# Token operands' low halves on VectorE, and a later load of the mixer's constants, in a two-layer decoder trunk

## The chip, the core and the metric

One core of one Trainium2 chip runs the whole kernel. The metric is the device time of one execution in microseconds; three runs of the kernel before are given by their median. The engines named here are TensorE (PE; its weight loads PEld), VectorE (DVE), ScalarE (ACT), GpSimd (POOL, which also issues transfers) and SyncE (SP, which here only issues transfers).

## The reference

Two layers, each a feed-forward sub-layer, a token mixer and a second feed-forward sub-layer, on x of 512 tokens by 1024 channels in float32:

```
h = rms_norm(x, g1);  x = x + 0.5 * (silu(h @ w_gate) * (h @ w_up)) @ w_down      # D_FF = 2816
h = rms_norm(x, g2);  q, k, v, u = split(h @ w_in)
    o = causal differential attention (4 heads, RoPE), rms_norm per head
    p = causal mean pooling of u over windows 2, 4, 8, 16, a linear map per group
    x = x + concat(o, p) @ w_out
h = rms_norm(x, g3);  x = x + 0.5 * (silu(h @ w_gate2) * (h @ w_up2)) @ w_down2
```

A final rms_norm follows the second layer.

## The kernel before, in words

Activations lie transposed: a partition is a channel, the free dimension holds the 512 tokens. Each matrix product is made of three matmuls of float32r halves (`mm3`, lines 95 to 97): a number t is split into hi, its rounding, and lo = t - hi, and the product is hi\*hi + hi\*lo + lo\*hi. So every operand, weight or token, needs a hi and a lo tile.

There are two ways to make them. `split` (lines 143 and 144) is a cast on ScalarE and a subtraction on VectorE. The way "by DMA" has ScalarE write -t, rounded, into lo, POOL issue a transfer that adds t to it as it lands, and ScalarE cast hi (lines 164 to 166 for weights, 359 to 361 for tokens). Weights come in blocks of 128 by 1024 through six raw tiles (`wraw`) and five hi and five lo tiles. `weights()` returns the next block and first starts the making of those up to four blocks ahead, with the loads of raw blocks three further ahead on SP's queue.

A feed-forward part (`ffn`) has 11 pairs of hidden blocks, in three groups of 4, 4 and 3; after each group a down projection of 8 blocks (`down`, 24 or 18 matmuls each) adds to x. The first pair of a part (the first two of the very first part) is `plain`: gate and up products straight from the normed x. During it the sum of squares becomes the row r, and `operands` makes the token operands of all other pairs. Those pairs, `mixed`, need seven products in place of eight: tokens are cut into halves and channels into even and odd, the weight blocks A11, A12, A21, A22 and sums of them (u1 to u4) are multiplied by b[1] to b[7], of which b[1] and b[2] are normed x itself (b11, b21), and the others b22 (b[3]) and the combinations e4, e5, e6, e7. A product is 24 matmuls of 128x256; the order is 1, 2, 6, 5, 7, 3, 4, with the weights A11, A12, u2, u1, u3, u4, A22. Products 1, 6, 7 and 4 add up in bank ps_a, 2 in ps_g, 5 and 3 in ps_c; between them ScalarE copies a bank out (p1, w, p5, with preference by `high_priority`) and VectorE adds it to another (g1, up2, g2). Product 6 goes on in ps_a and so needs p1 copied first. The blocks A11, A12 and A22 get their low halves by DMA; the sums get theirs by `split`.

Of the seven token operands b[1], b[2], b[6] and b[5] are made by `split`, and b[7], b[3], b[4] by DMA. `constants()` (lines 820 to 825) loads lam, cst (cosine and sine tables and pooling counts) and the causal mask on SP's queue and has VectorE cast the mask to bfloat16; it is called after the very first plain pair. The readers of these three are in `lambdas` and `mix`, after the first part.

The order of each engine's queue is fixed when the kernel is built, by the Tile scheduler: program order is the rank, and an instruction that is ready by the scheduler's estimate may go ahead of a better-ranked one that is not. On the chip every queue then runs strictly in that order.

Of the kernel before, what the change touches and what calls it, by code (L numbers as in the profile page):

```python
# [15 lines left out]
ALU = mybir.AluOpType  # L16
# [54 lines left out]
def trunk(ctx: ExitStack, tc: tile.TileContext, xT, gu1, dn1, win_qk, win_v, win_u, poolw, wout, gu2, dn2, small, lams, consts, outT):  # L71
    nc = tc.nc
# [8 lines left out]
    def arena(name, dt=F32R):  # L81
        return act.tile([P, 2, S], dt, tag="arena", name=name)
# [59 lines left out]
    def split(hi, lo, raw):  # L142
        nc.scalar.copy(hi, raw)  # L143
        nc.vector.tensor_sub(lo, raw, hi.bitcast(F32))  # L144
# [197 lines left out]
    def operands(norm, r):  # L342


        def quarter(name, dt=F32):
            return act.tile([P, 4, HS], dt, tag="arena", name=name)

        def h(odd, half):
            t = quarter("h")
            ts = slice(half * HS, (half + 1) * HS)  # L350
            for i in range(4):
                k = 2 * i + odd
                nc.vector.scalar_tensor_tensor(t[:, i, :], x[:, k, ts], sm[:, norm.gcol + k : norm.gcol + k + 1], r[:, ts], ALU.mult, ALU.mult)
            return t

        def parts(t, by_dma=False):
            hi, lo = quarter("bhi", F32R), quarter("blo", F32R)
            if by_dma:
                nc.scalar.mul(lo, t, -1.0)
                nc.gpsimd.dma_start(lo, t, accum_op=ALU.add)  # L360
                nc.scalar.copy(hi, t)
            else:
                split(hi, lo, t)
            return hi, lo

        b = {}
        b11 = h(0, 0)
        b[1] = parts(b11)
        b21 = h(1, 0)
        b[2] = parts(b21)  # L370
        b12 = h(0, 1)
        e5 = quarter("e5")
        nc.vector.tensor_sub(e5, b11, b12)
        b22 = h(1, 1)
        e6 = quarter("e6")
        nc.vector.scalar_tensor_tensor(e6, e5, -1.0, b22, ALU.mult, ALU.subtract)
        e4 = b21
        nc.vector.scalar_tensor_tensor(e4, e6, -1.0, b21, ALU.mult, ALU.subtract)
        b[6] = parts(e6)
        b[5] = parts(e5)  # L380
        e7 = b12
        nc.vector.tensor_sub(e7, b22, b12)
        b[7] = parts(e7, by_dma=True)
        b[3] = parts(b22, by_dma=True)
        b[4] = parts(e4, by_dma=True)
        return b

    def ffn(norm, l, nxt, first=None):
        st = {}
        hh, hl = [], []  # L390

        def hidden(u):

            hi, lo = arena("hhi"), arena("hlo")
            split(hi, lo, u)
            hh.append(hi)
            hl.append(lo)

        def plain(first, at):

            banks = [bank("ps_pl") for _ in range(4)]
            gates, u = [], pair32("u")

            def gated():
                if "b" not in st:
                    st["b"] = operands(norm, st["r"])
                for ps in banks[:2]:
                    s = single("silu")
                    nc.vector.tensor_mul(s, ps, st["r"])
                    nc.scalar.activation(s, s, AF.Silu)  # L410
                    gates.append(s)

            for q in range(8):
                if q == 0 and first:
                    first(banks[:2])
                if q == at:
                    st["rT"] = rms_cols(norm.ssum, 1.0 / D, pin=True)
                if q == at + 1:
                    st["r"] = rms_rows(st["rT"])
                if q < 4 and first:  # L420
                    continue
                blk, jj = divmod(q, 2)
                if jj == 0:
                    hi, lo = weights()
                ps = banks[blk // 2 * 2 + jj]
                for i in range(4):
                    c = slice((jj * 4 + i) * P, (jj * 4 + i + 1) * P)
                    mm3(ps, hi[:, c], lo[:, c], *norm.k(2 * i + blk % 2), blk % 2 == 0 and i == 0, blk % 2 == 1 and i == 3)
                if q == 6 and "r" in st:
                    gated()  # L430
            if not gates:
                gated()
            for jj in range(2):
                v = u[:, jj, :]
                nc.vector.scalar_tensor_tensor(v, banks[2 + jj], -1.0, st["r"], ALU.mult, ALU.mult)
                nc.vector.tensor_mul(v, v, gates[jj])
            hidden(u)

        def halves(t):
            return t.rearrange("p (j s) -> p j s", j=2)  # L440

        def mixed():

            b = st["b"]
            u = pair32("u")

            def product(q, ps, start):
                w = weights()
                for jj in range(2):
                    triples(ps[:, jj * HS : (jj + 1) * HS], w, b[q], jj, start and jj == 0, True, True)  # L450

            def copied(ps, name):
                t = single(name)
                with tc.high_priority(PRIO):
                    nc.scalar.copy(t, ps)  # L455
                return t

            a, g, c = bank("ps_a"), bank("ps_g"), bank("ps_c")
            product(1, a, True)
            p1 = copied(a, "p1")  # L460
            product(2, g, True)
            g1 = single("g1")
            with tc.high_priority(PRIO):
                nc.vector.tensor_add(g1, g, p1)
            nc.scalar.activation(g1, g1, AF.Silu)
            product(6, a, False)
            w = copied(a, "w")
            product(5, c, True)
            p5 = copied(c, "p5")
            product(7, a, False)  # L470
            up2 = single("up2")
            with tc.high_priority(PRIO):
                nc.vector.tensor_add(up2, a, p5)
            product(3, c, False)
            g2 = single("g2")
            with tc.high_priority(PRIO):
                nc.vector.tensor_add(g2, c, w)
            nc.scalar.activation(g2, g2, AF.Silu)
            product(4, a, False)
            with tc.high_priority(PRIO):  # L480
                nc.vector.tensor_mul(u[:, :, :HS], halves(a), halves(g1))
            nc.vector.tensor_mul(u[:, :, HS:], halves(up2), halves(g2))
            hidden(u)

        for hf, (q0, nq) in enumerate(PARTS):
            hh.clear()
            hl.clear()
            for q in range(q0, q0 + nq):
                if q >= plain_pairs(first):
                    mixed()  # L490
                elif q:
                    plain(None, -2)
                else:
                    plain(first, 6 if first else 2)
                    if first:
                        constants()

            def down(ps, n, part, ts=slice(0, S), midway=None):
                hi, lo = part
                for j in range(2 * nq):  # L500
                    if midway and j == nq:
                        midway()
                    c = slice(j * P, (j + 1) * P)
                    mm3(ps[:, ts], hi[:, c], lo[:, c], hh[j // 2][:, j % 2, ts], hl[j // 2][:, j % 2, ts], j == 0, j == 2 * nq - 1)
                nc.vector.scalar_tensor_tensor(x[:, n, ts], ps[:, ts], -0.5, x[:, n, ts], ALU.mult, ALU.add)  # L505

            tail = hf == len(PARTS) - 1
            last = tail and isinstance(nxt, Final)
            for n in range(KD - 2 if last else KD):
                down(bank("ps_dn"), n, weights())  # L510
                if tail:
                    nxt.add(n)
            if last:

                n = KD - 2
                parts = weights(), weights()
                first_half, second = slice(0, HS), slice(HS, S)
                for i in range(2):
                    down(bank("ps_dn"), n + i, parts[i], first_half)
                    nxt.add(n + i, first_half)  # L520
                down(bank("ps_dn"), n, parts[0], second, lambda: nxt.cols(first_half))
                nxt.add(n, second)
                down(bank("ps_dn"), n + 1, parts[1], second, nxt.rows)
                nxt.add(n + 1, second)
                nxt.finish(first_half)
                nxt.cols(second)
                nxt.rows()
                nxt.finish(second)
# [414 lines left out]
```

## Time and profile before

| | us |
|---|---|
| median of 3 runs (lowest, highest) | 1809.5 (1808.0, 1811.78) |
| profiled execution, its own time | 1807.46 |
| span of its trace | 1805.4 |
| TensorE busy | 1759.8 (97%) |
| VectorE busy | 1124.5 (62%) |
| ScalarE busy | 951.5 (53%) |
| GpSimd busy | 210.5 (12%) |

Busy shares are over the whole span; the mean granted TensorE clock was 0.988 of full speed. The profile names a group by line, engine, operation, and output tile <- input tiles. Buffer numbers are left out, so the token tiles b11, b21, b12 and b22 all appear as `h` (as do e7 and e4, which are written over b12 and b21), e5 and e6 as `e`, p1 and p5 as `p`. L143 and L144 are the two lines of `split` for all tiles.

### The profile page before, as it was taken

To read this page: it belongs to the slowest core of one execution; us is meant where nothing else is said; L and a number is where in the kernel's file an instruction comes from. 1 tells how busy PE (TensorE), PEld (TensorE's weight loads), DVE (VectorE), ACT (ScalarE), POOL (GpSimd) and SP (SyncE) were. 2 spreads that over 40 slices of the span, in tenths; PEclk is the share of its full clock that TensorE was granted. 3 is DMA by queue.
4 is the path that set the end of the run, shared out by engine and by line. 5 is a ranking of instruction groups with operands and counts; after the bars stand their busy time and mean duration, and the time that the engine had idled before them with its cause. 6 is when DMAs were issued, how large, how long until landed. Compare 5 with 4: busy or idle time off the path is not lost.

```text
span 1805.4 us, 26850 instructions
## 1 busy us (share of the span) xinstructions
PE 1759.8 (97%) x10936; PEld 1577.1 (87%) x10936; DVE 1124.5 (62%) x1495; ACT 951.5 (53%) x1298; POOL 210.5 (12%) x211
## 2 busy tenths in 40 slices
PE   9899999999999899999999999999999989999997
PEld 7889989877788889989889899898777879899896
DVE  5945646577967546646575466465788576465464
ACT  7635626545466526626565265264445666264453
POOL 1100001110022001001220010012100310010001
PEclk9999999999999999999999999999999999999999
DMA  9656746522236756737757466375122567376461
GB/s 277 164 141 148 190 103 162 151 65 74 70 102 134 181 134 155 188 89 166 186 119 185 116 164 187 94 167 149 39 74 71 149 126 193 90 181 173 115 155 47
DMA packets 73451, 246.95 MB, mean 137 GB/s; under 512 B 8048, under 2 KB 12784, under 8 KB 73328
## 3 DMA queue, kind: packets, MB, share of 16 engines
q1 hardware_dynamic: 52304, 169.18, 30.3%
q0 software_dynamic: 20880, 76.03, 23.6%
q8 instruction: 85, 1.39, 0.3%
q14 instruction: 38, 0.31, 0.1%
q10 hardware_dynamic: 144, 0.03, 0.0%
HBM read 236.82 MB, written 2.10 MB: 132 GB/s over the span
## 4 chain that ended last, share of the span: by engine, by line
PE 85%; DVE 6%; DMA 4%; issue 3%; ACT 1%; SPq 1%; POOL 1%; POOLq 0%; DVEq 0%; ACTq 0%
PE ps_dn L96 9%; PE ps_dn L95 9%; PE ps_dn L97 9%; PE ps_a L97 8%; PE ps_a L95 8%; PE ps_a L96 8%; PE ps_c L95 4%; PE ps_c L97 4%; PE ps_c L96 4%; PE ps_pr L95 2%; PE ps_pr L97 2%; PE ps_pr L96 2%; DMA wlo<-gu 2%; PE ps_g L95 2%; PE ps_g L96 2%
## 5 line engine op out<-in xcount | busy, mean ns | idle before, releaser
L143 ACT CAST whi<-wraw 128x1024 fp32r<-128x1024 f32 (+2 forms) x275 | 273.7, 997 | 458.1 <-PE ps_dn L96 143.8
L144 DVE TENSOR_TENSOR wlo<-wraw,whi 128x1024 fp32r<-128x1024 f32 (+2 forms) x275 | 317.5, 1156 | 114.1 <-ACT whi L143 113.3
L97 PE MATMUL ps_a<-bhi,wlo 128*128 128x256 f32 x1248 | 359.8, 288 | 15.5 <-DMA wlo<-gu 15.5
L95 PE MATMUL ps_a<-bhi,whi 128*128 128x256 f32 x1248 | 359.1, 288 | 5.3 <-ACT p L455 5.1
L96 PE MATMUL ps_a<-blo,whi 128*128 128x256 f32 x1248 | 359.7, 288 | 0.2
L96 PE MATMUL ps_dn<-hlo,whi 128*128 128x512 f32 (+1 forms) x716 | 276.6, 386 | 0.2 <-DVE hlo L144 0.2
L97 PE MATMUL ps_dn<-hhi,wlo 128*128 128x512 f32 (+1 forms) x716 | 276.0, 386 | 0.0
L95 PE MATMUL ps_dn<-hhi,whi 128*128 128x512 f32 (+1 forms) x716 | 275.7, 386 | 0.0
L97 PEld LDWEIGHTS ps_a<-bhi,wlo 128*128 128x128 f32 x1248 | 245.6, 197 | 16.3 <-DMA wlo<-gu 16.3
L95 PEld LDWEIGHTS ps_a<-bhi,whi 128*128 128x128 f32 x1248 | 245.3, 197 | 6.2 <-ACT p L455 5.3
L96 PEld LDWEIGHTS ps_a<-blo,whi 128*128 128x128 f32 x1248 | 245.2, 197 | 1.9 <-DMA blo<-h 1.0
L165 POOL DMA_DIRECT2D wlo<-gu x133 | 116.1, 875 | 1032.6 <-ACT wlo L164 800.0
L166 ACT CAST whi<-wraw 128x1024 fp32r<-128x1024 f32 x133 | 139.3, 1048 | 131.2 <-PE ps_dn L96 62.2
L505 DVE SCALAR_TENSOR_TENSOR x<-ps_dn,x 128x512 f32<-128x512 f32 (+1 forms) x98 | 66.6, 680 | 191.8 <-PE ps_dn L97 191.8
L95 PE MATMUL ps_c<-bhi,whi 128*128 128x256 f32 x624 | 177.2, 284 | 5.7 <-ACT bhi L143 5.7
L96 PE MATMUL ps_c<-blo,whi 128*128 128x256 f32 x624 | 177.4, 284 | 1.2 <-DMA blo<-h 1.0
L97 PE MATMUL ps_c<-bhi,wlo 128*128 128x256 f32 x624 | 176.9, 284 | 0.0
L96 PEld LDWEIGHTS ps_dn<-hlo,whi 128*128 128x128 f32 x716 | 134.5, 188 | 28.0 <-DVE hlo L144 1.6
L97 PEld LDWEIGHTS ps_dn<-hhi,wlo 128*128 128x128 f32 x716 | 134.5, 188 | 27.1
L95 PEld LDWEIGHTS ps_dn<-hhi,whi 128*128 128x128 f32 x716 | 134.5, 188 | 26.7
L164 ACT ACTIVATE wlo<-wraw 128x1024 fp32r<-128x1024 f32 x133 | 140.0, 1056 | 0.2 <-DMA wraw<-gu 0.2
L95 PEld LDWEIGHTS ps_c<-bhi,whi 128*128 128x128 f32 x624 | 120.2, 193 | 6.3 <-ACT bhi L143 6.3
(173 smaller groups left out, 3226.5 us busy)
## 6 DMA issues: line engine op xcount, KB each, us to landing
wraw<-gu SPq DMA_DIRECT2D x174, 512.0 KB, 3.8
wlo<-gu POOLq DMA_DIRECT2D x133, 512.0 KB, 7.1
wraw<-dn SPq DMA_DIRECT2D x64, 512.0 KB, 4.2
wraw<-dn SPq DMA_DIRECT2D x32, 384.0 KB, 3.4
wraw<-wqk SPq DMA_DIRECT2D x16, 512.0 KB, 3.6
wraw<-wo SPq DMA_DIRECT2D x16, 512.0 KB, 3.7
blo<-h POOLq DMA_DIRECT2D x12, 512.0 KB, 7.2
wraw<-wv SPq DMA_DIRECT2D x8, 512.0 KB, 3.7
```

The lines of the kernel that those rows point to most:

```text
L95: nc.tensor.matmul(out, a_hi, b_hi, start=start, stop=False, skip_group_check=more)
L96: nc.tensor.matmul(out, a_hi, b_lo, start=False, stop=False, skip_group_check=more)
L97: nc.tensor.matmul(out, a_lo, b_hi, start=False, stop=stop, skip_group_check=more)
L143: nc.scalar.copy(hi, raw)
L144: nc.vector.tensor_sub(lo, raw, hi.bitcast(F32))
L164: nc.scalar.mul(lo[:, :n], raw[:, :n], -1.0)
L165: nc.gpsimd.dma_start(lo[:, :n], src, accum_op=ALU.add)
L166: nc.scalar.copy(hi[:, :n], raw[:, :n])
L505: nc.vector.scalar_tensor_tensor(x[:, n, ts], ps[:, ts], -0.5, x[:, n, ts], ALU.mult, ALU.add)
```

## The change

The token operands b[7], b[3] and b[4] are made by `split` like the other four: ScalarE casts hi, VectorE subtracts. And `constants()` is called no longer after the first plain pair but after the four pairs of the first group, ahead of its down projection.

```
-        def parts(t, by_dma=False):
+        def parts(t):
             hi, lo = quarter("bhi", F32R), quarter("blo", F32R)
-            if by_dma:
-                nc.scalar.mul(lo, t, -1.0)
-                nc.gpsimd.dma_start(lo, t, accum_op=ALU.add)
-                nc.scalar.copy(hi, t)
-            else:
-                split(hi, lo, t)
+            split(hi, lo, t)
             return hi, lo
...
-        b[7] = parts(e7, by_dma=True)
-        b[3] = parts(b22, by_dma=True)
-        b[4] = parts(e4, by_dma=True)
+        b[7] = parts(e7)
+        b[3] = parts(b22)
+        b[4] = parts(e4)
...
                     plain(first, 6 if first else 2)
-                    if first:
-                        constants()
...
             last = tail and isinstance(nxt, Final)
+            if first and hf == 0:
+                constants()
             for n in range(KD - 2 if last else KD):
                 down(bank("ps_dn"), n, weights())
```

## Rows read from the trace of the kernel before

**Rows 1.** Page, part 1: busy us (share of span) and instructions by engine.

```profile
PE 1759.8 (97%) x10936; PEld 1577.1 (87%) x10936; DVE 1124.5 (62%) x1495; ACT 951.5 (53%) x1298; POOL 210.5 (12%) x211
```

**Rows 2.** TensorE's waits, whole span: total us, times, longest us.

```profile
PE ps_a L97 <- DMA wlo<-gu: 15.5, 4, 4.9
...
PE ps_c L95 <- ACT bhi L143: 5.7, 3, 1.9
...
PE ps_a L95 <- ACT p L455: 5.1, 1, 5.1
```

**Rows 3.** Windows, four places: length, busy by engine, granted clock, DMA share, GB/s.

```profile
58.64:85.85 27.21, 20.44 (x147) 20.09 (x145) 23.89 (x29) 21.00 (x26) 5.25 (x6) 0.87 0.91 212
571.53:601.23 29.70, 22.75 (x146) 21.79 (x145) 18.65 (x21) 18.42 (x21) 5.17 (x6) 0.83 0.74 162
930.35:959.89 29.54, 22.61 (x146) 21.56 (x145) 18.34 (x21) 18.41 (x21) 5.19 (x6) 0.83 0.74 163
1465.58:1493.86 28.28, 21.24 (x146) 20.32 (x145) 18.04 (x21) 18.52 (x21) 5.22 (x6) 0.88 0.78 170
```

**Rows 4.** TensorE timeline: start, length, what; first matmuls of two products.

```profile
604.11 0.28 PE L95 MATMUL ps_a<-bhi,whi 128*128 128x256 f32 x1
...
607.00 0.28 PE L95 MATMUL ps_c<-bhi,whi 128*128 128x256 f32 x1
```

**Rows 5.** Windows behind or around waits, columns as in rows 3.

```profile
63.90:69.80 5.90, 5.90 (x27) 5.90 (x28) 5.14 (x8) 5.68 (x8) 0.00 (x0) 0.50 1.06 211
78.30:85.85 7.55, 5.89 (x50) 5.68 (x48) 5.77 (x8) 3.56 (x4) 0.00 (x0) 1.00 1.03 238
592.94:599.00 6.06, 6.06 (x28) 6.06 (x29) 0.96 (x2) 1.04 (x1) 0.00 (x0) 0.50 0.83 206
932.50:937.20 4.70, 4.68 (x25) 4.59 (x26) 4.67 (x5) 3.34 (x4) 1.73 (x2) 0.64 0.38 60
```

**Rows 6.** VectorE timeline, first part; brackets: idle before it, what ended it.

```profile
38.61 1.23 DVE L175 TENSOR_TENSOR wsum<-wraw 128x1024 f32<-128x1024 f32 x1 [3.81 <-DMA wraw<-gu]
...
44.50 0.23 DVE L825 CAST maskb<-mask 128x128 bf16<-128x128 f32 x1 [4.66 <-DMA mask<-consts]
```

**Rows 7.** Timeline of ScalarE, first feed-forward part.

```profile
54.74 1.05 ACT L143 CAST bhi<-e 128x1024 fp32r<-128x1024 f32 x1 [3.88 <-DVE e L376]
...
63.27 0.57 ACT L455 COPY p<-ps_a 128x512 f32<-128x512 f32 x1
```

**Rows 8.** DMA issues: count, KB each, median us from issue to landing.

```profile
wlo<-gu POOLq DMA_DIRECT2D x133, 512.0 KB, 7.1
...
cst<-consts SPq DMA_DIRECT2D x1, 520.0 KB, 12.2
...
mask<-consts SPq DMA_DIRECT2D x1, 64.0 KB, 19.0
```

**Rows 9.** Timeline of ScalarE, second feed-forward part.

```profile
574.09 1.05 ACT L359 ACTIVATE blo<-h 128x1024 fp32r<-128x1024 f32 x1
...
578.47 0.59 ACT L455 COPY w<-ps_a 128x512 f32<-128x512 f32 x1 [1.44 <-PE ps_a L97]
...
582.27 2.02 ACT L164 ACTIVATE wlo<-wraw 128x1024 fp32r<-128x1024 f32 x2
```

**Rows 10.** Timeline of POOL, second feed-forward part.

```profile
583.63 1.81 POOL L165 DMA_DIRECT2D wlo<-gu  x2 [1.53 <-ACT wlo L164]
```

**Rows 11.** Tile blo: count, ns min/median/max, first and last start.

```profile
L359 ACT ACTIVATE blo<-h x12: 1046/1054/1063, 57.6 to 1473.7; 128x1024 fp32r<-128x1024 f32 x12
```

**Rows 12.** Timeline of VectorE, second feed-forward part.

```profile
572.74 2.35 DVE L144 TENSOR_TENSOR blo<-e,bhi 128x1024 fp32r<-128x1024 f32 x2
...
584.53 0.69 DVE L473 TENSOR_TENSOR up<-ps_a,p 128x512 f32<-128x512 f32 x1 [3.52 <-PE ps_a L97]
```

**Rows 13.** Windows, columns as in rows 3: first down projection; operands, second part.

```profile
106.00:120.00 14.00, 14.00 (x64) 11.59 (x63) 7.03 (x8) 2.61 (x3) 0.00 (x0) 1.00 0.35 100
560.00:580.00 20.00, 18.11 (x114) 16.78 (x113) 19.05 (x24) 12.24 (x15) 1.72 (x2) 0.91 0.31 72
```

## The prediction

> **What bounds the kernel now.** I read the engine totals first, then the list of what TensorE waited for, then windows over the stages where those waits lie, and last the queues of the other engines inside these stages.
>
> TensorE is busy for 1759.8 of 1805.4 us [rows 1], so all that an edit off TensorE can return is its idle time and its time at the lower clock. The list of its waits is short [rows 2]: the three long entries (15.5, 5.7 and 5.1 us) are all on ps_a and ps_c, the banks of the first seven-product pair of each of the four feed-forward parts, the place where the token operands are made. I take each such place from the end of product 2 to the end of the next pair's product 1: six products, 144 matmuls. At full rate 24 matmuls lie between 604.11 and 607.00, 0.120 us each [rows 4], so 144 need 17.3 us. The four places took 27.21, 29.70, 29.54 and 28.28 us [rows 3]: 9.9, 12.4, 12.2 and 11.0 us too long, 45.5 us together, about all of TensorE's idle time. What the change can win is in there.
>
> The loss is wait plus clock. [...] The same arithmetic gives 2.7 us behind the second part's 4.9 us wait (6.06 us, 28 matmuls) and 1.7 us behind a 1.9 us wait (4.70 us, 25 matmuls) [rows 5]. A wait of 1.7 us in the first part, behind 78.3, lowered nothing: its window has 5.89 of 7.55 us busy and shows 1.00.
>
> **First part: the constants.** VectorE stands 4.66 us before the cast of the mask [rows 6]. The mask took 19.0 us to land, behind cst, which took 12.2 [rows 8]. VectorE works in order, so the sums and operands behind the cast are late: ScalarE gets e6 only at 54.74, casts and negates without a gap, and comes to the copy p1, which product 6 needs, at 63.27 [rows 7]. Product 2 ended at 58.64, the edge of its window [rows 3]: that is the 5.1 us. Taking the cast away moves VectorE up by 4.66 us at least; at most by the 3.81 us more that it waited for wraw [rows 6], because that load was queued behind cst. I count on the lower end, since that load shares the transfers with others too. The three negations leave ScalarE as well, some 1.0 us each (2.02 for two [rows 9]). Together p1 could be ready 4.7 + 2.9 = 7.6 us earlier, at 55.7, before product 2 ends, so the wait and its 2.7 us of clock go. Against that, VectorE does three subtractions more before it comes to the weights' low halves of products 7 and 3, 1.18 us each (2.35 for two [rows 12]), 3.5 us; with 4.7 won its queue is 1.2 us earlier while TensorE is 5.1 earlier. So of the 9.9 something may stay: nothing at best, 3.9 of wait with 1.7 of clock at worst. The wraw load makes the better end likelier; I leave 1.4 and count **8.5 us**.
>
> **The place they go to.** cst, lam and mask are three issues on SP's queue, behind the loads already asked for, and they land while the down projection runs, where the transfers are 0.35 busy and VectorE 7.03 of 14 us [rows 13]. The cast then waits with VectorE's x updates and the down weights' low halves behind it. Those are prepared four blocks ahead; a block is 24 matmuls, 64 of which take 14 us, so 5.3 us. Even the old 19.0 us stays under 21 us. The readers of cst, lam and mask come with the mixer, after the whole part. Cost: zero. If that cover failed, because the cast stood ahead of the last hidden half of the pair before, it would be at most the old 4.66 us with 2.7 of clock, once.
>
> **Second part of the change: the low halves.** It removes 12 ScalarE negations (1054 ns [rows 11]), 12 POOL issues (0.9 us, from 1.81 for two [rows 10]) and 12 accumulating transfers of 512 KB, and adds 12 VectorE subtractions of 1.18 us. ScalarE's queue in the second feed-forward part goes: negation 574.09, cast, negation, copy w at 578.47, cast, negation, cast, copy p5, and only then, at 582.27, the negation of the weight A22 [rows 9]. POOL issues its transfer at 583.63 [rows 10]; product 4 has it at 592.94 and has waited 4.9 us, since 588.0 [rows 2, 5]. Without the three negations ScalarE has cast e7, b22 and e4 by 577.0 (574.09 + 3 x 0.97), and A22's negation, behind them by rank, needs no place behind w and p5. Taken at 577 to 579, with a microsecond of its own, 0.3 us handover and the median 7.1 us of such a transfer [rows 8], it lands at 585.4 to 587.4; with the 9.3 us that it took here, among three transfers of blo that no longer exist, at 589.6 at worst. TensorE asks at 588.0. So I take the wait and its clock as gone: 4.9 + 2.7 = **7.6 us** in the second part. The third place is 0.2 us shorter and the fourth 1.4 [rows 3], and their first waits are the same: **7.4** and **6.2**.
>
> What pays: the three subtractions on VectorE. It ends the last low half it makes of the operands today at 575.1, and idles 3.52 us before 584.53 [rows 12]. Straight on, the three end at 578.6; taken by turns with other work, at 582.2. TensorE wants them for products 7, 3 and 4: 588.0 for the last, 2.9 us earlier for each one before, 585.1 and 582.2, when by turns the first is done at 577.5 and the second at 579.8. Hidden by 4.7 to 9.4 us; without that cover, 3.5 us per part. The first waits of 1.9 us, on e5's cast, lie ahead of everything changed, and stay.
>
> [...] The rows show a wait of 1.7 us without a fall and one of 1.9 us with one [rows 5]. [...]
>
> **Sum.** 8.5 + 7.6 + 7.4 + 6.2 = 29.7 us. The profiled execution took 1807.5 us, 2.1 more than its span; 1807.5 - 29.7 = 1777.8. The median of the runs, 1809.5, lies 2.0 above it: 1780.
>
> **Rivals.** *A, A22 comes earlier, but not early enough.* ScalarE keeps its order and only closes up by 2.9 us: the transfer lands at 590.0, product 4 waits 2.0 us, with 1.7 of clock. Each later part then returns 7.6 - 3.7 = 3.9 us at most, some 3.4 on average: 8.5 + 10.2 = 18.7, so 1791. For it: w and p5 stand ahead of A22's negation now. Against it: the room before w.
>
> *B, the change does not reach that wait.* A22's negation stays behind p5, which waits for TensorE, and nothing moves in the later parts: 8.5 only, 1801. For it: 582.27 comes right behind p5. Against it: three instructions of better rank are gone.
>
> *C, slower: VectorE becomes the bound.* From 560 to 580 it is busy for 19.05 of 20 us [rows 13]. If the low halves of e7, b22 and e4 come so late that products 7, 3 and 4 each wait for their own, at 1.9 + 1.7 = 3.6 us, that is 10.8 per part: 4 x 10.8 - 29.7 = 13.5 us slower, 1823. It decides from the point where the first is later than 582.2, 4.7 us behind the turns above. The 3.52 us of idle time just behind the full stretch speak against it. [...]
>
> *D, better.* The new order also makes e5's cast and e6's low half earlier, and the three first waits go, 3 x 3.6 = 10.8: 1769. Nothing in the rows asks for it.
>
> **Chances and range.** Forecast 0.57 (alone, 1772 to 1787: the clock that the first waits may not cost, and the worst rest of the first part with a little of A), A 0.19, B 0.07, C 0.07, D 0.10. The range 1768 to 1797 takes in the forecast, A and most of D, and leaves out B and C. A measurement here can tell 0.2%, 3.6 us, from no change. Forecast, A, D and most of B are faster; a weak form of B or C can end level: faster 0.90, same 0.03, slower 0.07.
>
> **What would show it.** Right: no wait of VectorE for the mask before 50 us; the 5.1 us wait gone and the clock at 1.00 from 58 to 70; no wait for wlo of over 2 us in the four places, three waits of 1.9 us left; A22's negation ahead of the copy p5; the mask's cast past 90 us with no wait of TensorE near it. Wrong: waits of ps_a or ps_c for blo (C), for wlo (A, B), or one on ps_dn near 105 us.

## The result, and the profile after

The changed kernel takes 1782.55 us (median of 4 runs, 1777.02 to 1785.22) where the kernel before takes 1808.75 on the same chip: a ratio of 0.985, 95% interval 0.9822 to 0.9878, 1.5% faster. The prediction was 1780, with a range of 1768 to 1797. The profiled execution spans 1775.2 us, 30.2 less than the 1805.4 of before; the predicted sum was 29.7. That the sum fits so well is partly luck: the profiled execution (1777.02 us) is the fastest of the four, the medians lie 26.2 us apart, and the four places show errors that cancel.

TensorE's waits in the changed kernel, to be read against [rows 2]:

```profile
PE ps_c L95 <- ACT bhi L143: 5.7, 3, 1.9
PE ps_a L97 <- DMA wlo<-gu: 4.4, 2, 4.2
```

The 5.1 us for the copy p1 is off the list, though p1 itself is copied only at 60.08, after product 2 has ended at 58.51. TensorE's order at this place is another one: it takes 20 matmuls of product 5 (bank ps_c) first and comes to product 6 (bank ps_a) at 60.91.

```profile
60.08 0.56 ACT L450 COPY p<-ps_a 128x512 f32<-128x512 f32 x1
```

```profile
58.51 0.28 PE L95 MATMUL ps_c<-bhi,whi 128*128 128x256 f32 x1
...
60.91 0.28 PE L95 MATMUL ps_a<-bhi,whi 128*128 128x256 f32 x1
```

Of the four waits for A22's low half, 15.5 us, one of 4.2 us is left (the other is of 0.2). The three of 1.9 us are untouched.

The same four places as in [rows 3], again from the end of product 2 to the end of the next pair's product 1 (or to that point of the order in which TensorE now takes them); the columns are those of [rows 3]:

```profile
58.51:82.76 24.25, 19.51 (x147) 18.92 (x145) 17.80 (x22) 14.65 (x18) 2.62 (x3) 0.93 0.55 130
568.24:589.33 21.09, 19.20 (x147) 18.88 (x146) 19.49 (x22) 15.77 (x19) 2.57 (x3) 0.92 0.60 130
917.94:937.54 19.60, 17.71 (x147) 17.39 (x145) 19.39 (x22) 15.78 (x19) 2.59 (x3) 1.00 0.63 139
1443.66:1463.26 19.60, 17.71 (x146) 17.39 (x145) 19.40 (x22) 15.77 (x19) 2.60 (x3) 1.00 0.61 138
```

They return 3.0, 8.6, 9.9 and 8.7 us, together 30.2, the whole difference of the spans. Predicted were 8.5, 7.6, 7.4 and 6.2. The first place gave 5.5 us less than forecast, the three others 6.0 us more.

Why the later places gave so much is in ScalarE's queue, second feed-forward part; below it POOL's issue and the time of that transfer:

```profile
570.79 1.04 ACT L143 CAST bhi<-h 128x1024 fp32r<-128x1024 f32 x1
571.73 1.05 ACT L164 ACTIVATE wlo<-wraw 128x1024 fp32r<-128x1024 f32 x1
572.69 1.04 ACT L143 CAST bhi<-h 128x1024 fp32r<-128x1024 f32 x1
575.28 0.59 ACT L450 COPY w<-ps_a 128x512 f32<-128x512 f32 x1 [1.56 <-PE ps_a L97]
```

```profile
573.08 0.86 POOL L165 DMA_DIRECT2D wlo<-gu  x1 [25.10 <-DVE wlo L144]
```

```profile
wlo<-gu POOLq DMA_DIRECT2D x1, 512.0 KB, 7.8
```

A22's negation (the line at 571.73) stands ahead of the copy w and ahead of two of the three casts. It runs 3.5 us after the place begins; before, it ran 10.7 us after it (582.27 [rows 9] minus 571.53 [rows 3]). The mask's cast sits where the prediction put it, without a wait and with no wait of TensorE near it:

```profile
103.52 0.22 DVE L820 CAST maskb<-mask 128x128 bf16<-128x128 f32 x1
```

Of the loads, only those of lam and the mask have moved there. The largest one, cst, stands in SP's queue behind the weight loads of the start and is issued at 27.74; it takes 18.0 us and lands at 45.7, still in the first part. No engine reads it before the mixer, at 371.7:

```profile
27.74 0.50 SPq L817 DMA_DIRECT2D cst<-consts  x1
...
97.60 0.42 SPq L819 DMA_DIRECT2D mask<-consts  x1
```

What is left of the first place's loss is A22 again. First VectorE's rows, then ScalarE's, then a piece of the chain of work that ends with the matmul at 75.90:

```profile
51.48 3.50 DVE L144 TENSOR_TENSOR blo<-h,bhi 128x1024 fp32r<-128x1024 f32 x3
...
63.74 2.37 DVE L144 TENSOR_TENSOR wlo<-wraw,whi 128x1024 fp32r<-128x1024 f32 x2
```

```profile
63.87 1.05 ACT L166 CAST whi<-wraw 128x1024 fp32r<-128x1024 f32 x1 [1.75 <-PE ps_a L96]
...
66.72 2.96 ACT L164 ACTIVATE wlo<-wraw 128x1024 fp32r<-128x1024 f32 x3
```

```profile
68.08 7.77 DMA wlo<-gu
```

VectorE does the three new subtractions first and comes to the low halves of u3 and u4 only at 63.74, but TensorE has no wait for these. A22's negation comes at 66.72, and its transfer lands at 75.85. In ScalarE's queue that negation stands behind a cast that had to wait for TensorE's product 6 (63.87), and behind the copies w and p5 and one more cast; no row shows it waiting for VectorE. TensorE, no longer held by p1, asks for A22's low half 4.2 us before it has landed.

Last, the clock. The first window lies behind the 4.2 us wait, the others behind the three waits of 1.9 us:

```profile
75.90:80.50 4.60, 4.60 (x26) 4.60 (x27) 0.19 (x1) 0.41 (x1) 0.00 (x0) 0.63 0.83 165
570.70:575.00 4.30, 4.30 (x25) 4.29 (x25) 4.30 (x4) 3.02 (x4) 0.86 (x1) 0.62 0.29 56
920.40:924.70 4.30, 4.30 (x37) 4.29 (x36) 4.30 (x4) 4.22 (x6) 0.86 (x1) 1.00 0.30 53
1446.10:1450.40 4.30, 4.30 (x36) 4.27 (x36) 4.30 (x4) 4.22 (x6) 0.87 (x1) 1.00 0.28 51
```

The same wait of 1.9 us is followed by a granted clock of 0.62 once and of 1.00 twice: 25 matmuls in 4.30 us, against 37 and 36. That is the 1.5 us by which the second place is longer than the third.

### The profile page after: what moved, and what is told of

It reads as the page before. It is cut to its first block, busy times and chain, and to the rows that moved or that the text cites. A ratio compares the mean times of both kernels' runs of the same rounds, so it can differ in the third digit from the quotient of the medians.

```text
span 1775.2 us, 26832 instructions
## 1 busy us (share of the span) xinstructions
PE 1746.8 (98%) x10936; PEld 1565.7 (88%) x10936; DVE 1138.0 (64%) x1507; ACT 942.0 (53%) x1286; POOL 199.9 (11%) x199
## 4 chain that ended last, share of the span: by engine, by line
PE 92%; DVE 2%; DMA 2%; issue 1%; ACT 1%; SPq 1%; POOL 0%; POOLq 0%; DVEq 0%; ACTq 0%
PE ps_dn L96 9%; PE ps_dn L95 9%; PE ps_dn L97 9%; PE ps_a L97 8%; PE ps_a L96 8%; PE ps_a L95 8%; PE ps_c L95 4%; PE ps_c L96 4%; PE ps_c L97 4%; PE ps_pr L95 2%; PE ps_pr L97 2%; PE ps_pr L96 2%; PE ps_g L97 2%; PE ps_g L95 2%; PE ps_g L96 2%; PE ps_pl L97 2%
## 5 line engine op out<-in xcount | busy, mean ns | idle before, releaser
L97 PE MATMUL ps_a<-bhi,wlo 128*128 128x256 f32 x1248 | 354.7, 284 | 4.4 <-DMA wlo<-gu 4.4
L95 PE MATMUL ps_a<-bhi,whi 128*128 128x256 f32 x1248 | 354.6, 284 | 0.5 <-ACT whi L166 0.5
L96 PE MATMUL ps_a<-blo,whi 128*128 128x256 f32 x1248 | 354.8, 284 | 0.0
L97 PEld LDWEIGHTS ps_a<-bhi,wlo 128*128 128x128 f32 x1248 | 240.9, 193 | 4.9 <-DMA wlo<-gu 4.9
L95 PEld LDWEIGHTS ps_a<-bhi,whi 128*128 128x128 f32 x1248 | 240.8, 193 | 1.4 <-ACT whi L166 0.7
L96 PEld LDWEIGHTS ps_a<-blo,whi 128*128 128x128 f32 x1248 | 240.9, 193 | 0.8
```

The costliest lines, as they stand in the source:

```text
L95: nc.tensor.matmul(out, a_hi, b_hi, start=start, stop=False, skip_group_check=more)
L96: nc.tensor.matmul(out, a_hi, b_lo, start=False, stop=False, skip_group_check=more)
L97: nc.tensor.matmul(out, a_lo, b_hi, start=False, stop=stop, skip_group_check=more)
```

## The experiments

The theory to test: places 2 to 4 win because ScalarE's queue is freed for A22's negation, and place 1 keeps a wait because VectorE is late there. The main rival: it is the twelve transfers, not the queue. Experiments 3 and 4 test the places 2 to 4; experiments 5 and 6 show that the second half of the theory is not right as it stands. The table gives the length of the four places in the profiled execution of each kernel, from the same windows, and the median time. Each kernel was timed beside the kernel before on the same chip; those medians of before lie between 1808.1 and 1808.8.

| kernel | place 1 | 2 | 3 | 4 | median us | ratio to before (95%) |
|---|---|---|---|---|---|---|
| before | 27.21 | 29.70 | 29.54 | 28.28 | 1808.75 | |
| the change | 24.25 | 21.09 | 19.60 | 19.60 | 1782.55 | 0.985 (0.9822 to 0.9878) |
| 1 constants only | 23.18 | 29.58 | 29.28 | 28.32 | 1801.77 | 0.9957 (0.9941 to 0.9972) |
| 2 low halves only | 36.22 | 21.09 | 21.09 | 19.59 | 1789.07 | 0.9894 (0.9873 to 0.9914) |
| 3 negations kept | 24.94 | 25.96 | 24.49 | 26.54 | 1792.15 | 0.9914 (0.9897 to 0.993) |
| 4 transfers kept | 22.57 | 28.49 | 27.79 | 26.92 | 1800.36 | 0.9959 (0.9947 to 0.9971) |
| 5 low halves twice | 30.55 | 21.08 | 19.63 | 21.11 | 1795.53 | 0.9933 (0.9917 to 0.9949) |
| 6 first sums early | 19.80 | 19.61 | 19.60 | 21.08 | 1774.69 | 0.982 (0.9801 to 0.9839) |
| 7 e5, e6 first | 22.10 | 19.83 | 19.85 | 19.84 | 1773.25 | 0.9812 (0.9796 to 0.9828) |
| 8 both orders | 17.44 | 19.84 | 19.84 | 19.84 | 1769.11 | 0.979 (0.9773 to 0.9807) |
| 9 the change again | 25.12 | 19.59 | 19.58 | 21.09 | 1779.92 | 0.9847 (0.9832 to 0.9863) |
| 10 e7 before e4 | 17.28 | 19.85 | 19.84 | 19.83 | 1768.88 | 0.9785 (0.977 to 0.98) |

**1. The constants' move alone** (the kernel before, with `constants()` at its new place).

```diff
-                    if first:
-                        constants()
...
+            if first and hf == 0:
+                constants()
```

> Only the constants move; the three token low halves are made by DMA as before. Theory (the two parts act in different places): the mask wait of 4.66 us on VectorE and the 5.1 us wait of TensorE in the first place go, so that place falls from 27.2 to between 24 and 26 us, some wait for A22's low half staying; the three later places stay at 29.7, 29.5 and 28.3 us, each with its 4 to 5 us wait for wlo. Time 1804 to 1807 us against 1809. Rival 1 (as in the prediction's sum, the first place gives 8.5 us through the constants alone): 1800. Rival 2 (the copy p1 is late through ScalarE's negations, not through the mask): the 5.1 us wait stays at 2 us or more, 1808 to 1810.

It takes 6.4 us off the median and nothing from places 2 to 4. The median lies 2.2 us below the theory's range and 1.8 above rival 1. Place 1 goes from 27.21 to 23.18, and what is left there is a wait for A22's low half of 3.1 us and its clock. The copy p1 comes at 55.94, ahead of the end of product 2, as the prediction has it. The constants are worth 4.0 us in that place, under half of the first term of the sum.

**2. The low halves alone** (the changed kernel, with `constants()` back at its old place).

> Only the low halves change; the constants are loaded in the old place. Theory: the later places fall to 20 to 21 us each, with 1.9 us waits only, 26 us together; in the first place VectorE still stands some 4 to 5 us before the mask's cast, and TensorE waits there for p1, for A22 or for a low half, so that it stays at 25 to 28 us. Time 1780 to 1787 us. Rival (the later places need VectorE or the transfers as the moved constants leave them): they can't, since nothing of the constants is left after 50 us; if they stay above 24 us each, the theory of the separate places is wrong. Rival 2 (the three more subtractions behind the mask's cast make the first place worse than before): over 29 us there.

1789.07 lies 2 us above what was expected. Places 2 to 4 are those of the change. Place 1 is not: 36.22 us, 9 us worse than before, as the second rival had it (over 29), with two waits for VectorE; the longer one no other kernel here has.

```profile
PE ps_c L95 <- DVE u L430: 7.0, 1, 7.0
...
PE ps_c L97 <- DVE wlo L144: 2.1, 1, 2.1
```

With the mask's stall still in VectorE's queue (4.66 us here too), three more subtractions make TensorE wait 9.0 us for VectorE in the first part. So the two halves of the change aren't independent: the low halves cost 9.0 us at place 1 without the constants' move and 1.1 us with it (24.25 against 23.18).

**3. ScalarE's negations kept, the transfers gone** (the changed kernel; ScalarE also writes the negated operand into blo, which the split then overwrites).

```diff
+            if negated:
+                nc.scalar.mul(lo, t, -1.0)
             split(hi, lo, t)
...
-        b[7] = parts(e7)
+        b[7] = parts(e7, True)
```

(and so for b[3] and b[4])

> The changed kernel, but ScalarE still writes the three negations into the low-half tiles, where VectorE's subtraction then overwrites them: ScalarE's queue is as before, and the POOL issues and transfers of the token low halves are gone. Theory (the later waits came from A22's negation standing late in ScalarE's queue): its negation is again behind the copy p5, TensorE waits for wlo 3 to 5 us in each later place, places of 26 to 29 us, time 1800 to 1806 us. Rival (the three transfers were what delayed A22's): its transfer lands in some 7 us in place of 9.3 and the waits fall under 2 us, places of 21 to 23 us, 1783 to 1789 us.

**4. The transfers kept, the negations moved to VectorE** (experiment 1, with the three negations written by VectorE).

```diff
-                nc.scalar.mul(lo, t, -1.0)
+                nc.vector.tensor_scalar_mul(lo, t, -1.0)
                 nc.gpsimd.dma_start(lo, t, accum_op=ALU.add)
```

> The kernel before with the constants moved, and with the three token negations on VectorE in place of ScalarE; POOL issues and transfers of the token low halves stay. Theory (ScalarE's queue): A22's negation comes ahead of p5, some 5 us earlier than before, and the waits for wlo in the later places fall to 0 to 2.5 us, places of 20 to 23 us, time 1782 to 1791 us. Rival (the transfers): A22's transfer shares with three others and lands 9 us or more after its issue, waits of 3 to 5 us, places above 25 us, 1797 to 1805 us.

Neither gives the change's time: 1792.15 lies between the theory and the rival of experiment 3, and 1800.36 in the rival's range of experiment 4, though with shorter waits than the rival's. The two gains don't add up to the change's either. Places 2 to 4 take 87.2 us in experiment 1, 77.0 with the transfers gone, 83.2 with the negations gone from ScalarE, and 60.3 with both gone. The rows of the second part say why. ScalarE's row of A22's negation, first of experiment 3, then of experiment 4 (whose places begin at 569.00 and 567.00):

```profile
579.88 2.01 ACT L164 ACTIVATE wlo<-wraw 128x1024 fp32r<-128x1024 f32 x2
```

```profile
574.00 2.01 ACT L164 ACTIVATE wlo<-wraw 128x1024 fp32r<-128x1024 f32 x2
```

And the transfer of A22's low half from issue to landing (start and length, from the chain of work), again of 3 and then of 4:

```profile
581.25 6.57 DMA wlo<-gu
```

```profile
575.36 12.03 DMA wlo<-gu
```

With the negations kept, A22's negation comes 10.9 us after the place begins, as late as before, though its transfer takes 6.6 us instead of 9.3; TensorE waits 3.1 us instead of 4.9. With the transfers kept, the negation comes at 7.0 us, but its transfer then runs beside three of blo and takes 12.0 us; TensorE waits 2.2 us for A22 and three times 1.1 us for blo. A22 has to land by the time TensorE reaches it, and either cause left in place is enough to miss that. The change removes both: negation at 3.5 us, transfer 7.8. (In experiment 4 the negation is still 3.5 us later than in the change, so its wait isn't the work of the transfers alone.) The theory of the queue alone falls, and so does that of the transfers alone.

**5. The three low halves done twice** (the changed kernel; the second subtraction writes the same values).

```diff
             split(hi, lo, t)
+            if twice:
+                nc.vector.tensor_sub(lo, t, hi.bitcast(F32))
...
-        b[7] = parts(e7)
+        b[7] = parts(e7, True)
```

(and so for b[3] and b[4])

> The change with each of the three low halves' subtractions done twice on VectorE (the second overwrites the first with the same values): 1.14 us more for each, 3.4 us more of VectorE at each of the four places. Theory (VectorE has room at places 2, 3 and 4, since A22's negation stands behind the first mixed pair's wlo and not behind these subtractions; at place 1 the same three stand ahead of that wlo, so A22 comes later there by up to 3.4 us, and its wait of 4.2 us grows to about 7.6): 1785 to 1790, with the whole loss at place 1. Rival C of the prediction (VectorE sets the pace at every place): 3.4 us at each of four places and what the clock then costs, 1796 to 1805.

13.0 and 15.6 us slower than the two medians of the change, and 5.5 us past the theory's range, just short of the rival's. Places 2 to 4 are as in the change but for the clock behind the first wait, as the theory has it. Place 1 is 6.3 us longer, but not for the theory's reason: the wait for A22 is 4.19 us as in the change, not 7.6. What is new there is a wait for VectorE, for the low half of u1 in product 5:

```profile
62.68 0.58 PE L97 MATMUL ps_c<-bhi,wlo 128*128 128x256 f32 x1 [2.90 <-DVE wlo L144]
...
81.65 0.58 PE L97 MATMUL ps_a<-bhi,wlo 128*128 128x256 f32 x1 [4.19 <-DMA wlo<-gu]
```

VectorE, with 3.4 us of subtractions more, comes to that low half 4.1 us later (at 61.41 instead of 57.28), and the wait for A22 doesn't grow. So that wait is not set by how late VectorE is: ScalarE's negation follows the end of product 6, which is itself later here. The cast that waits for product 6 stands at 69.37 and the negation at 72.22, 2.85 us apart, as 63.87 and 66.72 in the change. Behind places 2 to 4 the cost comes back one pair later. A new entry in TensorE's waits:

```profile
PE ps_a L97 <- DVE wlo L144: 5.2, 3, 1.7
```

It is in the second mixed pair, behind each of these three places, where VectorE is late with the low half of a weight sum; the window from 595.75 to 620.12 took 24.37 us, against 20.16 for the same stretch of the change. So of 3.4 us added there, about 2.2 show as waits (1.74, and 0.44 for a high half), and most of the rest is clock (0.93 in that window). By that difference VectorE has some 1.2 us to spare behind the change (an estimate), and the prediction's 4.7 to 9.4 us was the room for the operands alone, not for what is queued behind them.

**6. The first mixed pair's sums early** (the changed kernel; the splits of u1, u3 and u4 get preference at place 1).

```diff
-            split(hi, lo, raw)
+            with tc.high_priority(PRIO if step[0] == "sum" and step[2] == 8 else 0):
+                split(hi, lo, raw)
```

> The change, with the splits of the first mixed pair's three weight sums put ahead in the order of ScalarE and VectorE, at place 1 alone. Theory (what is left of the A22 wait at place 1, 4.2 us, is due to VectorE coming late to the last wlo, behind which A22's negation is placed): the wait falls under 1.5 us and the 26 products behind it run at the full clock more often; place 1 takes 19.6 to 22 us instead of 24.3, and the time is 1776 to 1780. Rival (A22's transfer, or its landing in memory, sets the wait whatever the order): the wait stays at 3.5 us or more, 1781 to 1785.

The wait for A22 is gone from place 1, which takes 19.80 us at a clock of 1.00, 4.5 less. ScalarE's first negation, A22's, now stands at 59.91 instead of 66.72:

```profile
58.95 1.04 ACT L166 CAST whi<-wraw 128x1024 fp32r<-128x1024 f32 x1 [1.83 <-PE ps_g L96]
59.91 1.06 ACT L164 ACTIVATE wlo<-wraw 128x1024 fp32r<-128x1024 f32 x1
```

The rival falls: the order sets this wait, and not the transfer. Of the theory, the wait and the place come out as expected, and the time 1.3 us below its range. Its reason, VectorE's lateness, is not what the rows show. Here the negation follows the cast of A22's high half at once; in the change that cast stands at 58.59 and the negation 8.1 us later, behind a cast that waits for product 6. So what was left at place 1 was the position of A22's negation in ScalarE's queue, fixed when the kernel is built; why the scheduler put it there was not traced.

**7. e5's and e6's halves ahead of e4 and e7 on VectorE** (the changed kernel).

```diff
-        e4 = b21
-        nc.vector.scalar_tensor_tensor(e4, e6, -1.0, b21, ALU.mult, ALU.subtract)
         b[6] = parts(e6)
         b[5] = parts(e5)
+        e4 = b21
+        in_order(nc.vector.scalar_tensor_tensor(e4, e6, -1.0, b21, ALU.mult, ALU.subtract))
         e7 = b12
-        nc.vector.tensor_sub(e7, b22, b12)
+        in_order(nc.vector.tensor_sub(e7, b22, b12))
```

> The change, with the two computations of e4 and e7 on VectorE put behind the halves of e6 and e5. Theory (the 1.89 us wait of the first product of places 2 to 4 is for ScalarE's copy of bhi, which waits for VectorE's e6 and e5 and not for its own queue): each of these three waits falls by about 1 us, 3 us in all, and the clock behind them falls less often, up to 5 us more: 1774 to 1780. Rival (ScalarE's own queue sets these waits, or e4 and e7 are then late for the third product): 1781 to 1786, with waits of 1.9 us in the same place or behind it.

The time is nearer the theory (0.8 us below its range), and the waits are those of the rival:

```profile
PE ps_a L96 <- DVE blo L144: 4.2, 3, 1.4
...
PE ps_c L95 <- ACT bhi L143: 1.4, 3, 0.5
```

The 1.9 us at each place became 0.5 and, at product 7, 1.4, the same sum. Yet the clock stays at 1.00 in all three places, and each takes 19.84 us, where a wait of 1.9 us in one piece leaves 19.6 or 21.1. What is won at places 2 to 4 is that the clock never falls, and at place 1 another order (22.10).

**8. Both orders together.**

> Both orders together (the first mixed pair's sums ahead at place 1, and e4 and e7 behind the halves of e6 and e5). Theory: the two gains add, since they are waits at different places: 1770 to 1776, faster than the change alone by 6 to 12 us. Rival (one of the two stays): 1776 to 1782.

```profile
58.00:75.44 17.44, 17.44 (x146) 17.37 (x145) 17.08 (x22) 13.83 (x17) 2.62 (x3) 1.00 0.73 167
562.20:582.04 19.84, 18.00 (x147) 17.46 (x145) 19.64 (x21) 15.44 (x18) 2.57 (x3) 1.00 0.70 152
```

Place 1 runs without a gap (144 x 0.120 = 17.3 us), the others as in experiment 7. 1769.11 us, in the range of the theory: 13.4 and 10.8 us below the two medians of the change.

**9. The change in a second execution.**

> The change as it is, profiled in a second execution. Theory (the first waits of places 2 to 4 last 1.89 us in each execution, and what differs between executions is whether the 23 products behind them run at half clock or at full, 1.5 us in each place): the waits are the same to 0.1 us, the span differs from that of the first profile by the places at half clock, about 1.5 us each, and by little else; median 1780 to 1784. Rival (the executions differ in other stretches): the three places and the first take the same time as in the first profile, and the span differs elsewhere.

```profile
568.86:588.45 19.59, 17.70 (x146) 17.39 (x145) 19.39 (x22) 15.76 (x19) 2.57 (x3) 1.00 0.62 139
...
1443.54:1464.63 21.09, 19.20 (x147) 18.89 (x146) 19.48 (x22) 15.76 (x19) 2.60 (x3) 0.92 0.57 125
```

The first waits are 1.89 us again. This time the second place keeps the clock and the fourth loses it. The theory holds for the places and only for a part of the difference: the span is 2.3 us longer, the four places 0.8 us (85.38 against 84.54), and the rest lies elsewhere. The median is 1779.92, just below the lower edge of what was expected.

**10. e7 before e4** (experiment 8, with the two computations exchanged).

> Both orders together, and e7 before e4 on VectorE. Theory (the 1.39 us wait that is left at the third product of places 2 to 4 is for the low half of e7, which stands one computation of 1.14 us too late): the wait falls to about 0.3 us, 3.3 us in all: 1764 to 1768. Rival (the copy on ScalarE, or VectorE's weight sums ahead of that low half, sets the wait): 1768 to 1771, the wait stays above 1.2 us.

The rival holds: the waits are 1.4 us still and the time is the same. VectorE's rows show what is ahead of e7's low half now:

```profile
567.94 1.23 DVE L176 TENSOR_TENSOR wraw<-wraw 128x1024 f32<-128x1024 f32 x1
569.08 1.22 DVE L144 TENSOR_TENSOR blo<-h,bhi 128x1024 fp32r<-128x1024 f32 x1
```

e7 is ready 1.1 us earlier, but a weight sum (L176) still stands ahead of its low half, and ScalarE's cast of it hasn't moved either: behind the copy w, 5.46 us after the place begins, in experiments 8 and 10 alike. Which of the two would be the next limit was not tried.

## Why the prediction was right, and where it was not

**First part, 8.5 us: mis-sized.** It measured 3.0 us in one execution and 2.1 in the other. The mechanism of its first half was right for the constants: the mask's wait and p1's 5.1 us are gone, the clock is 1.00 there (the 2.7 us of clock that the prediction took for that wait are the 5.90 us at a granted clock of 0.50 of [rows 5] less 27 x 0.120), and VectorE even moved up at the better end, since the wait of 3.81 us for wraw went too. (p1 ready at 55.7 is what experiment 1 shows, 55.94; in the change it is copied at 60.08, and the wait is gone because product 5 goes first.) The step that failed is "I leave 1.4" for what stays behind. At worst it had 3.9 us of wait with 1.7 of clock, and 4.2 us of wait and about 1.5 of clock stayed (26 matmuls in 4.60 us). The size is near that worst end, but the cause is another: the prediction derived it from VectorE's low halves of products 7 and 3, for which TensorE doesn't wait, and what stayed is the wait for A22, which was 1.7 us before and which the prediction did not carry forward. The arithmetic closes: the matmul that needs A22's low half began at 80.24 before, after a wait of 1.7, and at 75.90 now, 4.3 us earlier; TensorE came to it 6.9 us earlier, so the wait grew by 2.5. e6's cast had moved up by 8.8 us (45.92 instead of 54.74 [rows 7]), but A22's negation by only 4.1 (66.72 instead of 70.86), since ScalarE's queue has it behind product 6 (experiments 5 and 6). By experiment 1 and the change the constants give 4.0 us at this place and the low halves take 1.1 back; by experiment 6 an order that puts the sums first returns 4.5.

**The constants' new place at nothing: right in the cost, not in the whole account.** The cast at 103.52 waits for nothing. But that all three land while the down projection runs held for lam and the mask alone; cst was under way from 27.74 to 45.7, and what paid was that VectorE's cast moved and, by the order of SP's queue, that cst no longer stood ahead of the last weight loads of the start (before, it was issued at 22.44 and the next of these loads at 23.72).

**Second part of the change, 7.6, 7.4 and 6.2 us: right in its mechanism, too small.** 8.6, 9.9 and 8.7 were measured in one execution, 10.1, 10.0 and 7.2 in the other. A22's negation came earlier than the 577 to 579 that the prediction counted on: measured from the start of the place, 3.5 us instead of 5.5 to 7.5. Two things were left out of the terms, or not in full: the falls of the clock behind the first waits, which did not all come back, and small waits for blo, such as the 1.0 us in the fourth part of before. What the prediction told as the work of ScalarE's queue is, by experiments 3 and 4, the work of the queue and of the transfers together; the prediction had the transfers only as its worst end (9.3 us among the three of blo).

**The first waits of 1.9 us: they stayed, their price did not.** The prediction took each of them to cost 1.7 us of clock, the 4.70 us of [rows 5] less 25 x 0.120, before the change and after it; its band of 1772 to 1787 left room for waits that cost less. In the nine profiled executions that keep this wait (before, the change twice, and experiments 1 to 6; 27 waits of 1.89 us) the clock fell behind 17 and held behind 10. So the length of the wait alone doesn't settle what it costs; what else does is not shown. The kernel before could not show it: there, and in experiment 1, the clock fell behind all six, in the seven other executions behind 11 of 21. Whether that is chance is not shown.

**The subtractions hidden: right, with less to spare than counted.** Experiment 5 shows 1.2 us or so of room, one pair later than the prediction looked. Rival C, that VectorE becomes the bound, is no story from far off: experiment 2 is that rival at place 1, and experiment 5 at every part. VectorE is busy for 19.4 of 19.6 us at places 3 and 4 of the change, ScalarE for 15.8. But ScalarE held what TensorE needed next, and work moved from it to the busier engine paid.

**The sum** came out at 30.2 against 29.7 because 5.5 us too much at the first place met 6.0 too little at the others. Rivals A and B did not happen at places 2 to 4 (no wait for A22 there); a form of A did at place 1, where the prediction's sign against it, no wait for wlo of over 2 us, failed. One reading of the rows was wrong without a consequence: the 45.5 us lost at the four places are not "about all of TensorE's idle time". TensorE stood idle for 27.7 us of them (114.73 us of length, 87.05 busy), the rest was lost while it was busy, most of it at the low clock (granted 0.83 to 0.88 over the places [rows 3]), and 17.9 us of its idle time lie elsewhere.

## What to carry to other kernels

When an instruction is removed from an engine's queue, look for what comes early because of it and what still delays that: here the weight's negation and its transfer both had to move, and removing either cause alone returned a fraction. When one stall goes, work out anew every arrival behind it, each from the queue that holds it: a cast that VectorE's stall held up came 8.8 us earlier, A22's negation in ScalarE's queue only 4.1, and the place got 3.0 us shorter. And where waits are down to 2 us, how they are split can matter as much as their sum, since here the clock fell behind one wait of 1.89 us in 17 of 27 cases, and behind two of 0.5 and 1.4 us in none of 9.

## What the runs showed of the hardware

- The same wait of 1.89 us was followed by a half-rate stretch (14 to 18 matmuls at 0.21 to 0.23 us instead of 0.12; 1.5 us in all, 1.7 to 1.9 in the kernel before and experiment 1) in 17 of 27 cases, and in one kernel at other places in one execution than in another. Split into 0.5 and 1.4 us, with some 6 us of matmuls between, it was followed by none in 9 of 9 places (experiments 7, 8 and 10).
- An accumulating transfer of 512 KB, A22's, took 6.6 us (experiment 3, second part) and 7.8 to 8.9 us (the change, places 2 to 4) without the three of blo. With them it took 9.3 us in the second part of the kernel before and 12.0 us in experiment 4 (575.36 to 587.39), where TensorE's waits for the three of blo ended at 576.46, 580.68 and 584.87, all within it.
